# Splitting part of the weights into high and low parts by DMA

## The chip, the cores and the metric

One core of one Trainium2 chip. The metric is the device time of one execution in microseconds (us); lower is better. The engines are PE (matrix multiply), DVE (VectorE), ACT (ScalarE), POOL (GpSimd) and SP (SyncE, which here only issues DMAs). They run side by side, each takes its own instructions in a fixed order, and they wait for each other through semaphores.

## What is computed

One transformer layer over 512 tokens of width 1024. Of the reference, cut to what matters here:

```python
proj = rms_norm(x, g_mix) @ w_in
(q_n, kc_n, vc_n, ks_n, vs_n, kw_n, vw_n, gate_n,
 q_m, k_m, v_m, gate_a, gate_b) = jnp.split(proj, IN_CUTS, axis=-1)
y_nsa = nsa_mixer(q_n, kc_n, vc_n, ks_n, vs_n, kw_n, vw_n, gate_n, ...)
y_moba = moba_mixer(q_m, k_m, v_m, ...)
merged = sigmoid(gate_a) * (y_nsa @ w_up_nsa) + sigmoid(gate_b) * (y_moba @ w_up_moba)
x = x + merged @ w_out
gate, up = jnp.split(rms_norm(x, g_ffn) @ w_ffn_in, 2, axis=-1)
x = x + (silu(gate) * up) @ w_ffn_out
x = x + sigmoid(rms_norm(x, g_ple) @ w_ple_gate) * (p @ w_ple_proj)
```

All inputs are fp32. The weights that matter here are those of `gate_a` and `gate_b` (2048 columns of `w_in`; `ga` in the kernel) and `w_up_moba` (`um`).

## The kernel before

**Three products for one.** PE multiplies in fp32r, a shortened fp32. To keep the precision, each operand is split into a high part, the value rounded to fp32r, and a low part, the rest. A product is then high x high + low x high + high x low: `tmm` (L358 to L363) issues three matmuls of 128x128 weights by 512 tokens, L361 with the weights' high part `wh`, L362 with `wh` again and the activations' low part, L363 with the weights' low part `wl`.

**Weight units.** The weights come in 144 units of up to 128x1024 (512 KB), in the order of the list `units` (L206 to L219). Units 30 to 33 are `vm` (values of MoBA), 34 to 44 are `ga` 8 to 15 and 0 to 2, 45 to 48 are `um`, 49 to 53 are `ga` 3 to 7, 54 on are `un`. The class `Weights` (L54 to L101) prepares them: `load` issues a DMA on SP's queue into one of three `wr` buffers (L67), `parts` takes one of three `wh` and one of three `wl` buffers, writes `wh` with an ACT copy that rounds to fp32r (L84) and `wl = wr - wh` with a DVE subtraction (L85). `get` hands out the next unit, splits up to one unit ahead and loads up to five ahead.

**What runs beside what.** First come the projections in natural layout (`qm` to `vm`). Then attention (`attention`, L777) is woven with a filling of 20 units, 34 to 53: `gates` (L536) multiplies eight `tmm` per `ga` unit, ends in a DVE product (L541) and an ACT tanh (L542); `up` (L903) does the same for `um`. The weave (L933 to L937) gives 0.95 filling steps per attention step, later 0.65. An attention job has score matmuls (L790, L791), a DVE pass that masks and takes the bound (L793), the exponential on ACT (L795), a DVE or ACT scaling (L808, L810), transposes on PE (L818), a split of their result by ACT and DVE (L827, L828) and the product with the values (L837, L842). After it come the up projection of NSA, the output projection, the feed-forward part and the last gate.

**Order.** The program text gives priorities; the Tile framework, with `schedule_with_timeline_sim=True` (L1116), fixes the order of each engine's instructions when the program is built, from the priorities and a simulated timeline. So an instruction can stand earlier in its engine's queue than the text has it: ACT's copy into a `wh` buffer stands where the buffer comes free. Which unit an instruction belongs to is known from the built program, where the buffers are numbered (`wh34`) and whose order of matmuls the trace repeats; the trace itself leaves the numbers out.

```python
# L358 to L363, of tmm
T.matmul(o, wh[:, sl], h, start=start, stop=False)
T.matmul(o, wh[:, sl], l, start=False, stop=False)
T.matmul(o, wl[:, sl], h, start=False, stop=stop)
# L933 to L937
fill = chain(gates(8, 16), gates(0, BEFORE_UM), up("um", YM, up_moba_done), gates(BEFORE_UM, 8))
run(weave(weave(att, fill, *FILL_RATE), side, 0.2))
```

Of the kernel before, what the change touches and what calls it, by code (L numbers as in the profile page):

```python
# [10 lines left out]
F32 = mybir.dt.float32  # L11
F32R = mybir.dt.float32r
I32 = mybir.dt.int32
AF = mybir.ActivationFunctionType
OP = mybir.AluOpType
# [38 lines left out]
class Weights:  # L54
    def __init__(self, nc, pool, units):
        self.nc, self.pool, self.units = nc, pool, units
        self.raw, self.done = {}, {}
        self.n_raw = self.n_split = self.n_get = 0
        self.depth = 2

    def load(self, upto):
        while self.n_raw < min(upto, len(self.units)):
            i = self.n_raw
            src, n = self.units[i][1], self.units[i][2]
            t = self.pool.tile([128, 1024], F32, name=f"wr{i}", tag="wr", bufs=3)
            for a, b in self.pieces(i, n):
                self.nc.sync.dma_start(t[:, a:b], src[:, a:b])  # L67
            self.raw[i] = t
            self.n_raw += 1

    def pieces(self, i, n):
        return [(0, n // 2), (n // 2, n)] if i == 0 else [(0, n)]

    def parts(self):
        i = self.n_split
        self.load(i + 1)
        self.n_split += 1
        n = self.units[i][2]
        t = self.raw.pop(i)
        h = self.pool.tile([128, 1024], F32R, name=f"wh{i}", tag="wh", bufs=3)  # L80
        l = self.pool.tile([128, 1024], F32R, name=f"wl{i}", tag="wl", bufs=3)
        self.done[i] = (h, l)
        for a, b in self.pieces(i, n):
            self.nc.scalar.activation(h[:, a:b], t[:, a:b], AF.Copy)  # L84
            self.nc.vector.tensor_sub(l[:, a:b], t[:, a:b], h[:, a:b].bitcast(F32))  # L85
            yield
# [8 lines left out]
    def get(self, key):  # L95
        i = self.n_get
        assert self.units[i][0] == key, (self.units[i][0], key)
        self.n_get += 1
        self.split(i + self.depth)
        self.load(i + 6)  # L100
        return self.done.pop(i)  # L101

# [1018 lines left out]
```

## Time and profile before

| | |
|---|---|
| median of 3 runs | 863.8 us (863.54 to 864.02) |
| the profiled execution | 863.29 us |
| its span, first to last instruction | 861.4 us |
| busy: PE, DVE, ACT, POOL | 843.4, 532.2, 391.3, 139.2 us |
| HBM read | 79.64 MB |

PE is busy for 98% of the span. Matmuls are pipelined: one of 512 tokens has a record of some 390 ns, while the next starts some 230 ns after it. A wait is the idle time of an engine just before an instruction, with what released it. The stretch of the change is attention, about 160 to 376 us; the weights of units 34 to 36 are split before it, from 148 us on.

### The profile page before, as it was taken

Reading aid. Unit: us, or ns where it says so; the run is one execution under the profiler, and the core shown is the slowest. Engines: PE = TensorE matmul, PEld = TensorE weight load, DVE = VectorE, ACT = ScalarE, POOL = GpSimd, SP = SyncE. Lnnn points to the kernel's source line nnn. Section 1 sums busy time; section 2 is a strip of 40 time slices with the busy share of each in tenths; the row PEclk is TensorE's granted clock in tenths of the full one; section 3 lists DMA queues with packets and bytes.
Section 4 is the critical chain, followed back from the end, with each engine's and each line's share of the span. In section 5 each row is a group of like instructions: output and inputs, shape, how many; then the busy total and the mean of one; then the engine's idle time right before and its main releaser. Section 6 shows DMA issues by size and latency. Waiting matters only on the chain.

```text
span 861.4 us, 11012 instructions
## 1 busy us (share of the span) xinstructions
PE 843.4 (98%) x4169; PEld 708.5 (82%) x4169; DVE 532.2 (62%) x944; ACT 391.3 (45%) x708; POOL 139.2 (16%) x140
## 2 busy tenths in 40 slices
PE   9999999999999999999999999999999999999997
PEld 7878798888788888787888888888888888888886
DVE  6777766878976988749536555555555433233354
ACT  6455545877776877634423222233333222233421
POOL 2735443000000000024321111111111101010100
PEclk9999999999999999999999999999999999999999
DMA  9433525423211111116323333333323333333221
GB/s 328 153 99 98 162 73 142 129 64 89 84 49 50 50 49 36 63 49 216 102 76 121 98 98 97 99 98 97 95 91 94 84 109 87 93 110 97 98 99 49
DMA packets 26996, 85.58 MB, mean 99 GB/s; under 512 B 3392, under 2 KB 3904, under 8 KB 26944
## 3 DMA queue, kind: packets, MB, share of 16 engines
q1 hardware_dynamic: 26016, 82.78, 30.3%
q10 hardware_dynamic: 928, 2.11, 1.0%
q8 instruction: 32, 0.52, 0.3%
q14 instruction: 20, 0.16, 0.1%
HBM read 79.64 MB, written 2.10 MB: 95 GB/s over the span
## 4 chain that ended last, share of the span: by engine, by line
PE 84%; DVE 8%; ACT 2%; POOL 2%; DMA 2%; issue 1%; SPq 0%; DVEq 0%; ACTq 0%; POOLq 0%
PE fg L361 5%; PE fu L362 5%; PE fg L362 5%; PE fob L361 5%; PE fob L362 5%; PE fu L361 5%; PE fg L363 5%; PE fu L363 5%; PE fob L363 5%; PE ga L361 3%; PE ga L362 3%; PE ga L363 3%; PE pt L818 3%; DVE wl L85 2%; PE pgb L361 2%; PE pv L842 2%
## 5 line engine op out<-in xcount | busy, mean ns | idle before, releaser
L84 ACT ACTIVATE wh<-wr 128x1024 fp32r<-128x1024 f32 (+2 forms) x145 | 147.4, 1019 | 310.3 <-PE fu L362 73.6
L85 DVE TENSOR_TENSOR wl<-wr,wh 128x1024 fp32r<-128x1024 f32 (+2 forms) x145 | 196.2, 1357 | 106.0 <-ACT wh L84 105.4
L361 PE MATMUL fg<-x2h,wh 128*128 128x512 f32 x176 | 68.6, 390 | 0.0
L361 PE MATMUL fu<-x2h,wh 128*128 128x512 f32 x176 | 68.6, 390 | 0.0
L363 PE MATMUL fg<-x2h,wl 128*128 128x512 f32 x176 | 68.5, 389 | 0.0
L363 PE MATMUL fu<-x2h,wl 128*128 128x512 f32 x176 | 68.5, 389 | 0.0
L363 PE MATMUL fob<-HH,wl 128*128 128x512 f32 x176 | 68.5, 389 | 0.0
L362 PE MATMUL fu<-x2l,wh 128*128 128x512 f32 x176 | 68.5, 389 | 0.0
L362 PE MATMUL fg<-x2l,wh 128*128 128x512 f32 x176 | 68.5, 389 | 0.0
L362 PE MATMUL fob<-HL,wh 128*128 128x512 f32 x176 | 68.5, 389 | 0.0
L361 PE MATMUL fob<-HH,wh 128*128 128x512 f32 x176 | 68.5, 389 | 0.0
L1008 POOL TENSOR_TENSOR u<-zg,u 128x512 f32<-128x512 f32 x22 | 29.8, 1352 | 199.9 <-DVE u L1006 191.4
L361 PE MATMUL ga<-xh,wh 128*128 128x512 f32 x128 | 53.6, 419 | 0.0
L362 PE MATMUL ga<-xl,wh 128*128 128x512 f32 x128 | 50.3, 393 | 0.0
L363 PE MATMUL ga<-xh,wl 128*128 128x512 f32 x128 | 50.2, 393 | 0.0
L793 DVE CUSTOM_DVE_ANT_0 p<-sb,big_mask 128x512 f32<-128x512 f32 (+2 forms) x96 | 44.9, 484 | 7.3 <-PE sb L791 7.1
L1006 DVE SCALAR_TENSOR_TENSOR u<-fu,rb 128x512 f32<-128x512 f32 x22 | 15.2, 690 | 53.6 <-PE fu L363 53.6
L944 POOL TENSOR_TENSOR GT<-GT,GT 128x512 f32<-128x512 f32 x8 | 14.7, 1856 | 190.5 <-DVE GT L943 190.5
L245 POOL TENSOR_TENSOR ssum<-ssum,sqx 128x512 f32<-128x512 f32 x14 | 22.1, 1575 | 139.1 <-ACT sqx L244 139.1
L818 PE MATMUL pt<-ident,p 128*128 128x128 f32 x240 | 38.2, 274 | 2.8 <-DVE pw L828 2.7
L828 DVE TENSOR_TENSOR pw<-pt,pw 128x512 fp32r<-128x512 f32 x48 | 32.6, 684 | 10.7 <-ACT pw L827 10.3
L361 PEld LDWEIGHTS fu<-x2h,wh 128*128 128x128 f32 x176 | 33.1, 188 | 6.9
(590 smaller groups left out, 1993.5 us busy)
## 6 DMA issues: line engine op xcount, KB each, us to landing
wr<-fi SPq DMA_DIRECT2D x44, 512.0 KB, 3.4
wr<-ga SPq DMA_DIRECT2D x16, 512.0 KB, 3.5
wr<-fo SPq DMA_DIRECT2D x16, 512.0 KB, 3.5
wr<-wo SPq DMA_DIRECT2D x8, 512.0 KB, 3.6
wr<-pg SPq DMA_DIRECT2D x8, 512.0 KB, 3.4
wr<-fo SPq DMA_DIRECT2D x8, 384.0 KB, 3.2
xin<-xT SPq DMA_DIRECT2D x8, 256.0 KB, 5.5
xn<-xN SPq DMA_DIRECT2D x4, 512.0 KB, 7.8
```

Of the source, the lines that this page charges most:

```text
L84: self.nc.scalar.activation(h[:, a:b], t[:, a:b], AF.Copy)
L85: self.nc.vector.tensor_sub(l[:, a:b], t[:, a:b], h[:, a:b].bitcast(F32))
L245: G.tensor_tensor(ssum, ssum, q, op=OP.add)
L361: T.matmul(o, wh[:, sl], h, start=start, stop=False)
L362: T.matmul(o, wh[:, sl], l, start=False, stop=False)
L363: T.matmul(o, wl[:, sl], h, start=False, stop=stop)
L793: V.tensor_tensor_reduce(out=p, in0=o, in1=big_mask[:, 512 - n:512], op0=OP.add, op1=OP.min, scale=1.0, scalar=3.0e38, accum_out=st["m"][: ...
L818: last = T.transpose(b[:, off:off + 128], st["p"][:, P_OFF[qt] + kb * 128:P_OFF[qt] + kb * 128 + 128], ident)
L828: V.tensor_sub(pl, b[:, :off], ph.bitcast(F32))
L842: T.matmul(o, job["v"](kb), st.pop(("pl", kb))[:, cols], start=False, stop=job["last"] and kb == 2)
L1006: V.scalar_tensor_tensor(u, bu, 2.0, rb1, op0=OP.mult, op1=OP.mult)
L1008: G.tensor_tensor(u, zg, u, op=OP.mult)
```

## The change

For the units named `ga` and `um` (20 of 144, `by_dma`) `load` issues nothing. `fetch`, one unit further ahead than the split, takes the `wh` and `wl` buffers and issues a DMA on POOL's queue from the fp32 weights into the fp32r `wh`, which casts on the way. `parts` then writes `wl = -wh` with an ACT pass of the same size as the old copy, and issues a second DMA on POOL's queue that adds the weights to `wl` (`accum_op=OP.add`). The DVE subtraction is gone for these units. `get` calls `fetch` for one unit more than is split. `wr` buffers are no longer used by these units, so later units can be loaded into them earlier.

```diff
@@ class Weights
     def load(self, upto):
         while self.n_raw < min(upto, len(self.units)):
             i = self.n_raw
+            if self.by_dma(i):
+                self.n_raw += 1
+                continue
...
+    def by_dma(self, i):
+        return i < len(self.units) and self.units[i][0][0] in ("ga", "um")
+
+    def fetch(self, upto):
+
+        while self.n_high < min(upto, len(self.units)):
+            i = self.n_high
+            if self.by_dma(i):
+                src, n = self.units[i][1], self.units[i][2]
+                h = self.pool.tile([128, 1024], F32R, name=f"wh{i}", tag="wh", bufs=3)
+                l = self.pool.tile([128, 1024], F32R, name=f"wl{i}", tag="wl", bufs=3)
+                self.nc.gpsimd.dma_start(h[:, :n], src)
+                self.high[i] = h, l
+            self.n_high += 1
+
     def parts(self):
         i = self.n_split
+        if self.by_dma(i):
+            self.fetch(i + 1)
+            self.n_split += 1
+            src, n = self.units[i][1], self.units[i][2]
+            h, l = self.done[i] = self.high.pop(i)
+            self.nc.scalar.activation(l[:, :n], h[:, :n].bitcast(F32), AF.Copy, scale=-1.0)
+            self.nc.gpsimd.dma_start(l[:, :n], src, accum_op=OP.add)
+            yield
+            return
         self.load(i + 1)
         self.n_split += 1
+        self.n_high = max(self.n_high, i + 1)
...
         self.split(i + self.depth)
+        self.fetch(self.n_split + 1)
         self.load(i + 6)
```

## Rows read from the trace of the kernel before

**Rows 1.** The page's busy times: engine, us, share of the span, instructions.
```profile
PE 843.4 (98%) x4169; PEld 708.5 (82%) x4169; DVE 532.2 (62%) x944; ACT 391.3 (45%) x708; POOL 139.2 (16%) x140
```
**Rows 2.** Busy time by stretch, 148 to 376 us; the first line names the columns.
```profile
core 0: us, PE busy (x) PEld busy (x) DVE busy (x) ACT busy (x) POOL busy (x), PEclk, DMA share, GB/s
...
180.00:200.00 20.00, 19.44 (x112) 16.30 (x111) 17.88 (x54) 14.70 (x34) 0.74 (x1) 1.00 0.27 80
...
sum 228.00, PE 223.44 PEld 190.18 DVE 180.53 ACT 162.72 POOL 2.22; mean PE 18.62 PEld 15.85 DVE 15.04 ACT 13.56 POOL 0.18
```
**Rows 3.** PE's waits, 160 to 376 us: waiter, releaser, us in total, times, longest.
```profile
PE pt L818 <- DVE pw L828: 2.7, 5, 1.5
PE sb L790 <- DVE am__2543 L793: 0.6, 1, 0.6
PE sb L790 <- DVE am__1754 L793: 0.5, 1, 0.5
PE sb L790 <- DVE am__3097 L793: 0.4, 1, 0.4
```
**Rows 4.** Instructions by line and form, 160 to 376 us, of DVE and ACT.
```profile
L85 DVE TENSOR_TENSOR wl<-wr,wh 128x1024 fp32r<-128x1024 f32 x20 | 24.4, 1218 | 2.5 <-ACT wh L84 2.4
...
L84 ACT ACTIVATE wh<-wr 128x1024 fp32r<-128x1024 f32 x20 | 21.1, 1055 | 10.5 <-PE ga L362 10.5
```
**Rows 5.** Timeline of PE, the matmuls behind four waits: start, us, what, [idle before].
```profile
160.03 0.50 PE L790 MATMUL sb<-KM,QM 128*128 128x512 f32 x1 [0.45 <-DVE am__1754 L793]
...
196.19 0.41 PE L818 MATMUL pt<-ident,p 128*128 128x128 f32 x2 [0.56 <-DVE pw L828]
...
234.55 0.41 PE L818 MATMUL pt<-ident,p 128*128 128x128 f32 x2 [1.45 <-DVE pw L828]
...
252.66 0.66 PE L818 MATMUL pt<-ident,p 128*128 128x128 f32 x4 [0.32 <-DVE pw L828]
```
**Rows 6.** Timeline of DVE ahead of those four waits.
```profile
158.29 1.22 DVE L85 TENSOR_TENSOR wl<-wr,wh 128x1024 fp32r<-128x1024 f32 x1
...
188.49 1.23 DVE L85 TENSOR_TENSOR wl<-wr,wh 128x1024 fp32r<-128x1024 f32 x1
...
230.10 0.69 DVE L770 TENSOR_TENSOR yf<-pv,yt 64x512 f32<-64x512 f32 x1 [0.37 <-ACT yt L766]
...
248.86 1.22 DVE L85 TENSOR_TENSOR wl<-wr,wh 128x1024 fp32r<-128x1024 f32 x1
```
**Rows 7.** DMAs: issue (ns min/median/max, us), time to landing (us), size.
```profile
L67 SPq DMA_DIRECT2D wr<-ga x10: 327/328/328, 168.7 to 307.2; - x10
...
DMA to landing us min/median/max: 3.2/3.3/4.5
...
169.22 0.51 ACTq L454 DMA_DIRECT2D k2M<-KM  x1
...
k2M<-KM ACTq DMA_DIRECT2D x4, 256.0 KB, 4.3
```
**Rows 8.** Timeline of POOL, its longest instruction between 140 and 200 us.
```profile
146.15 1.65 POOL L393 TENSOR_TENSOR hf__1532<-ss__1531,half_neg 128x8 f32<-128x8 f32 x1 [9.32 <-DVE ss__1531 L392]
```
**Rows 9.** Timeline of ACT, the copies into `wh` of units 34, 37 and 38.
```profile
148.20 1.06 ACT L84 ACTIVATE wh<-wr 128x1024 fp32r<-128x1024 f32 x1 [0.30 <-PE vm L353]
...
166.39 1.06 ACT L84 ACTIVATE wh<-wr 128x1024 fp32r<-128x1024 f32 x1
...
177.07 1.06 ACT L84 ACTIVATE wh<-wr 128x1024 fp32r<-128x1024 f32 x1 [0.88 <-PE ga L362]
```
**Rows 10.** Timeline of PE, the first matmul with `wl` of units 34, 37 and 38.
```profile
161.20 0.39 PE L363 MATMUL ga<-xh,wl 128*128 128x512 f32 x1
...
182.62 0.39 PE L363 MATMUL ga<-xh,wl 128*128 128x512 f32 x1
...
191.53 0.39 PE L363 MATMUL ga<-xh,wl 128*128 128x512 f32 x1
```
**Rows 11.** One line of the source, L810: one job's three scalings, ns min/median/max.
```profile
L810 DVE TENSOR_SCALAR p<-p,as__2839 x3: 285/347/414, 265.1 to 265.5; 128x128 f32<-128x128 f32 x1, 128x256 f32<-128x256 f32 x1, 128x384 f32<-128x384 f32 x1
```

## What the change should do to the time

> **What bounds the kernel now.** I read the busy times first: PE is busy for 843.4 of 861.4 us [rows 1], so only 18 us of the whole span can be won by shortening waits. The change touches 20 weight units (numbers 34 to 53 in the list `units`), all used beside attention. The second view is the table by stretch [rows 2]: at 180 to 200 us DVE is busy for 17.88 of 20 us, ACT for 14.70, POOL for 0.74, the DMA engines for a share of 0.27, and the granted clock is 1.00, so the clock is no part of this. PE is nevertheless the engine that lacks time: from 148 to 376 us it is busy for 223.44 of 228.00 us. The third view lists what PE waited for there [rows 3]: 2.7 + 0.6 + 0.5 + 0.4 = 4.2 us, every piece released by a DVE instruction. That is the ceiling of what a relieved DVE can give back.
>
> **What it removes.** Per unit, one load into `wr` on SP's queue, one ScalarE copy into `wh` and one VectorE subtraction into `wl`. A subtraction takes 1218 ns [rows 4], so 20 of them are 24.4 us of DVE time. What of it lies on the path? I went to each wait of PE and looked back along DVE to the last moment at which DVE stood idle. Three waits have a `wl` subtraction in the unbroken run that leads to them: 0.45 us at 160.03, 0.56 at 196.19 and 0.32 at 252.66 [rows 5], with the subtractions at 158.29, 188.49 and 248.86 [rows 6]. Each wait is shorter than the 1.2 us taken out ahead of it, so each goes: 0.45 + 0.56 + 0.32 = **1.3 us**. The longest wait, 1.45 us at 234.55 [rows 5], has none in its run, which starts at 230.10 behind ACT's `yt` [rows 6]; I leave it standing. What is late next is the same DVE work without the subtraction (score bounds at L793, products at L828), and PE itself. So the gain lies between 0 and 4.2 us; I take 1.3 because that part has its cause in the rows. SP loses 20 issues of loads that were there ahead of their use; nobody waits for that.
>
> **What it adds.** ScalarE keeps one pass per unit: `l = -h` over 128x1024 replaces `h = w` over 128x1024, 1055 ns each [rows 4]; net zero, and no gain, since the shape is the same. POOL gets two DMA issues per unit, 40 in all. The cast and the addition each read 512 KB from HBM where one load did: 20 x 512 KB = 10.5 MB more, over a stretch of some 200 us in which the DMA engines have three quarters of their time free [rows 2].
>
> The price is delay. Before, `wh` of a unit is written as soon as its buffer (one of three) is free, and `wl` right behind it. After: the buffer is free, POOL issues the cast, it lands, ACT writes `l`, POOL issues the addition, it lands. Nothing in this trace is issued by POOL, casts or adds, so each term has two ends:
> - An issue on POOL: 0.33 us is what SP's takes, 0.51 what ACT's takes [rows 7], 1.65 POOL's longest instruction near there [rows 8]. I take 0.5, the nearest in kind.
> - The cast: a plain 512 KB load lands after 3.2 us at best and 3.3 at the median; above, a load and an on-chip copy one after the other, 3.3 + 4.3 = 7.6 us [rows 7]. I take 3.3, since it reads and writes what the plain load does.
> - The addition must also read its destination: the same ends, and I take the middle, 5.4, as neither row is nearer.
> - ACT's pass: 1.06.
>
> Sum: 0.5 + 3.3 + 1.06 + 0.5 + 5.4 = **10.8 us**. With the lower ends it is 0.33 + 3.2 + 1.06 + 0.33 + 3.2 = 8.1, with the upper ends 1.65 + 7.6 + 1.06 + 1.65 + 7.6 = 19.6.
>
> How long may it take? From the moment the buffer is free to the unit's first matmul with `wl` (L363). ACT's pass of before starts when the buffer comes free, so its start marks the first of these. For unit 34 that is 148.20 to 161.20: **13.0 us**; for unit 37, 166.39 to 182.62: 16.2; for unit 38, 177.07 to 191.53: 14.5 [rows 9, 10]. The other 17, worked out in the same way, have 15.9 us or more. So 10.8 us is hidden everywhere, with 2.2 to spare at unit 34, and 19.6 is not. Where the cover is gone, PE stands at L363 until the addition lands.
>
> POOL's queue is in order: an addition waits there for ACT, and behind it stands the next unit's cast. That cast needs a buffer that comes free about 10 us after the one before (166.39, 177.07 [rows 9]), so it loses nothing. POOL's own work in the stage is 0.74 us at 180 to 200 [rows 2] and the tail of the projections at 146.15 [rows 8]. In ACT's queue the pass now waits for a landing, and behind it stand the exponentials and evacuations of attention: that is the first rival.
>
> There is one more thing on DVE that POOL's issues could meet: scaling the probabilities (L810) takes 285, 347 and 414 ns for 128, 256 and 384 columns [rows 11], so some 65 ns per further 128 columns, where a `wl` subtraction takes 1218 / 8 = 152 per 128 [rows 4]. The three add up to 1.05 us, once per attention job. If each held one POOL issue back by its whole length, both issues of a unit would make the chain 10.8 + 2.1 = 12.9 us, still inside 13.0. The Trainium skill, SBUF — State Buffer, section "SBUF: two separate sides", says that POOL can't write a DMA's descriptors while DVE works in a mode that uses two ports, and gives about 620 ns for a transfer alone against 3100 ns beside such work. By that, as an estimate 2.5 us more per transfer, the chain would be 15.8 us; no run here shows it yet.
>
> **Against the clock of the runs.** The profiled execution took 863.29 us, 1.9 more than its span, and the median of the runs is 863.8. Forecast: 863.29 - 1.3 = 862.0 for such an execution, 863.8 - 1.3 = **862.5** for the median.
>
> **Rivals.**
> - *ACT stands.* The order on each engine is fixed when the program is built, by a planner that assumes a landing time for the cast. If the chip's is later by d, ACT stands d at each of 20 passes with the exponentials behind it, and PE waits for those. For it: ACT is busy for 14.70 of 20 us [rows 2], so it has about 2.7 us free per unit of some 10. Against it: the buffer comes free 13 us or more before the unit is due, so the pass need not be early in the queue. With d = 1 us ACT loses 20 us; between none and all of it reaches PE, half is 10: 863.8 - 1.3 + 10 = 872.5, slower. It decides from 3.0 us reaching PE, a d of 0.3 us.
> - *The addition lands late.* From a chain of 13.0 us on, PE waits at unit 34. At the upper end: 19.6 - 13.0 = 6.6 there, 19.6 - 16.2 = 3.4 at unit 37, 19.6 - (14.5 + 3.4) = 1.7 at unit 38: 11.7 us, 874.2, and some more at units of 16 to 17 us. For it: adding is the one operation without a near row. Against it: 2.2 us to spare at the tightest place, 3.7 and more elsewhere.
> - *DVE holds POOL up*, at 2.5 us per issue in place of the 1.05 of the rows: 15.8 - 13.0 = 2.8 at unit 34 and 15.8 - 14.5 = 1.3 at unit 38, 863.8 - 1.3 + 4.1 = 866.6. The rows speak against it: no run of L810 is that long.
> - *All DVE waits go.* With 24 us less on DVE the planner may place the rest so that all of [rows 3] vanishes: 863.8 - 4.2 = 859.6.
>
> That the change doesn't do what it says would be a cast that copies the bits as they are: then `l` is zero and the time is that of the forecast, since every instruction still runs.
>
> **How the numbers follow.** Chances: forecast 0.47 (own range 861 to 864), ACT stands 0.27, addition late 0.13, DVE holds POOL up 0.05, all waits go 0.08. A measurement of this kernel can tell about 0.2% from no change, 1.7 us. The forecast's 1.3 us is inside that: of its 0.47, 0.36 is "same", 0.10 faster (a little more than 1.3 won) and 0.01 slower. ACT stands: 0.22 slower, 0.05 same. Addition late: 0.10 slower, 0.03 same. DVE holds POOL up: slower. All waits go: faster. Together: faster 0.18, same 0.44, slower 0.38. The range, 860.3 to 873, leaves out the full gain of 4.2 us (0.06), the upper part of ACT's case (0.08) and of the late addition (0.05).
>
> **What would show it.** In the changed trace: no `wl` subtraction for `ga` and `um`, 24 us less DVE, and PE's waits for DVE in the stage down from 4.2 to about 2.9 us. ACT's pass waiting for a DMA, with PE idle behind exponentials, is the first rival; PE waiting for a DMA at L363 the second; long POOL issues beside L810 the third. I am wrong if the two landings of a unit add up to more than 11 us, or if ACT's waits for the casts sum to more than 6 us.

## The result: 868.9 us, 0.56% slower, and the profile after

| | before, same chip | after |
|---|---|---|
| median | 863.7 us | 868.9 us (868.61 to 869.94) |
| ratio to before, 95% interval | 1 | 1.0056 (1.0040 to 1.0072) |
| span of the profiled execution | 861.4 us | 866.7 us |
| HBM read | 79.64 MB | 90.13 MB |

The forecast was 862.5 with a range to 873.0. The time is inside the range, but on the other side of before. The stage of the change, from the first `ga` unit to the last, holds the whole loss: what follows it runs 5.3 us later than before, in unchanged spacing, to the end.

Page of after, the busy times and the two new DMAs (512 KB each; the last column is the us from issue to landing):

```profile
PE 846.3 (98%) x4169; PEld 709.6 (82%) x4169; DVE 511.9 (59%) x924; ACT 390.7 (45%) x708; POOL 168.4 (19%) x180
...
wh<-ga POOLq DMA_DIRECT2D x16, 512.0 KB, 3.9
wl<-ga POOLq DMA_DIRECT2D x16, 512.0 KB, 5.4
```

Against [rows 1] DVE has 20 instructions and 20 us less, POOL 40 instructions more, ACT the same number; 10.5 MB more are read. So the change does what it says.

PE's waits in after, 160 to 376 us, the stretch of [rows 3], with all the rest that the view shows:

```profile
PE pv L866 <- ACT pw L856: 2.9, 1, 2.9
PE ga L392 <- DMA wl<-ga: 1.3, 1, 1.3
PE pt L847 <- DVE PC L758: 0.7, 1, 0.7
PE pt L847 <- DVE pw L857: 0.6, 3, 0.2
PE sb L819 <- DVE am__2529 L822: 0.4, 1, 0.4
PE sb L819 <- DVE am__3747 L822: 0.4, 1, 0.4
PE sb L819 <- DVE am__3580 L822: 0.2, 1, 0.2
PE pt L847 <- DVE as__2530 L832: 0.2, 1, 0.2
PE sb L819 <- DVE am__2097 L822: 0.2, 1, 0.2
```

The seven rows released by DVE sum to 2.7 us where [rows 3] has 4.2. Two rows are new: 2.9 us behind ACT, once, and 1.3 us behind a DMA, once. ACT's own waits for the casts, same stretch:

```profile
ACT wl L99 <- DMA wh<-ga: 7.8, 9, 2.4
ACT wl L99 <- DMA wh<-um: 0.5, 1, 0.5
```

A stand is the time in which ACT waits for a cast with its next work queued behind. Timelines of after: ACT at its two long stands, and from the second of them to L856, the split of attention's transposed probabilities; then PE's wait for that, and PE's other new wait:

```profile
223.98 1.06 ACT L99 ACTIVATE wl<-wh 128x1024 fp32r<-128x1024 f32 x1 [2.35 <-DMA wh<-ga]
...
234.06 1.06 ACT L99 ACTIVATE wl<-wh 128x1024 fp32r<-128x1024 f32 x1 [2.06 <-DMA wh<-ga]
235.02 0.61 ACT L801 ACTIVATE YMh<-yf 128x512 fp32r<-128x512 f32 x1
235.54 0.49 ACT L824 ACTIVATE p<-p,am__2529 128x256 f32<-128x256 f32 x1
...
236.53 1.09 ACT L856 ACTIVATE pw<-pt 128x512 fp32r<-128x512 f32 x2
...
237.19 0.62 PE L866 MATMUL pv<-pw,VM 128*128 128x512 f32 x1 [2.87 <-ACT pw L856]
...
161.40 0.50 PE L392 MATMUL ga<-xh,wl 128*128 128x512 f32 x1 [1.27 <-DMA wl<-ga]
```

The passes at 223.98 and 234.06 are those of units 42 and 43. Behind the second are queued a copy (L801), two exponentials (L824) and then the copy L856 that PE waits for. The first, though it stood longer, has no wait of PE behind it: PE was busy for all of 217 to 228 us. The stretch that holds this, by windows (columns as in [rows 2]):

```profile
220.00:240.00 20.00, 16.50 (x86) 13.64 (x85) 13.96 (x43) 12.71 (x29) 2.30 (x3) 0.94 0.67 142
240.00:260.00 20.00, 19.29 (x107) 16.39 (x107) 12.83 (x37) 14.57 (x33) 2.83 (x4) 0.98 0.40 86
```

The granted clock, 1.00 in every such window of before, is 0.94 and then 0.98. The record of the clock behind it: half (1.2 for 2.4 GHz) for 3.4 us from 237.4 on, that is, from 0.2 us after the end of PE's 2.87 us of idle. Work lost there: (0.06 + 0.02) x 20 = 1.6 us. Before is not free of this: of its 20 executions beside the first four experiments, 12 have a mean granted clock of 0.998 and a mean span 1.6 us longer than the six at 1.00, so the 1.6 us lost here is not in full a loss against before's median.

The whole attention stage of both, 140 to 385 us (before, then after):

```profile
140.00:385.00 245.00, 240.24 (x1314) 203.94 (x1314) 188.67 (x517) 171.59 (x402) 5.84 (x8) 1.00 0.21 65
...
140.00:385.00 245.00, 237.27 (x1290) 200.15 (x1289) 165.78 (x492) 168.43 (x399) 32.72 (x46) 0.99 0.48 108
```

So of the 5.3 us, 240.24 - 237.27 = 3.0 is idle of PE, 1.6 the half clock, and 0.7 remains, which was not traced further (the matmuls come in another order, at other spacings).

### The profile page after: what moved, and what is told of

Read it like the earlier page. It is cut to its first block, busy times and chain, and to the rows that moved or that the text cites. A ratio compares the mean times of both kernels' runs of the same rounds, so it can differ in the third digit from the quotient of the medians.

```text
span 866.7 us, 11013 instructions
## 1 busy us (share of the span) xinstructions
PE 846.3 (98%) x4169; PEld 709.6 (82%) x4169; DVE 511.9 (59%) x924; ACT 390.7 (45%) x708; POOL 168.4 (19%) x180
## 3 DMA queue, kind: packets, MB, share of 16 engines
HBM read 90.13 MB, written 2.10 MB: 106 GB/s over the span
## 4 chain that ended last, share of the span: by engine, by line
PE 79%; DVE 6%; issue 6%; DMA 4%; POOL 3%; ACT 2%; SPq 0%; POOLq 0%; DVEq 0%; ACTq 0%
PE fg L390 5%; PE fg L392 5%; PE fu L392 5%; PE fob L391 5%; PE fu L391 5%; PE fg L391 5%; PE fob L390 5%; PE fob L392 5%; PE fu L390 5%; PE pt L847 2%; PE ga L392 2%; PE ga L390 2%; PE ga L391 2%; PE pgb L390 2%; PE pgb L392 2%
## 5 line engine op out<-in xcount | busy, mean ns | idle before, releaser
L112 ACT ACTIVATE wh<-wr 128x1024 fp32r<-128x1024 f32 (+3 forms) x125 | 126.3, 1014 | 304.6 <-PE fu L391 69.5
L113 DVE TENSOR_TENSOR wl<-wr,wh 128x1024 fp32r<-128x1024 f32 (+3 forms) x125 | 171.7, 1378 | 105.3 <-ACT wh L112 104.9
L392 PE MATMUL fg<-x2h,wl 128*128 128x512 f32 x176 | 68.5, 389 | 0.0
L392 PE MATMUL fu<-x2h,wl 128*128 128x512 f32 x176 | 68.5, 389 | 0.0
L392 PE MATMUL fob<-HH,wl 128*128 128x512 f32 x176 | 68.5, 389 | 0.0
L392 PE MATMUL ga<-xh,wl 128*128 128x512 f32 x128 | 50.6, 396 | 1.3 <-DMA wl<-ga 1.3
L391 PEld LDWEIGHTS fg<-x2l,wh 128*128 128x128 f32 x176 | 33.1, 188 | 6.9
L390 PEld LDWEIGHTS fob<-HH,wh 128*128 128x128 f32 x176 | 33.0, 188 | 6.9
```

## The experiments

Each ran beside before on the same chip; ratios are to that. Three theories stand behind the expectations: **A**, ACT stands at the cast's landing; **B**, the planner's new order costs it, whatever lands when; **C**, the low parts land late.

**The passes on POOL.** In `parts`:

```diff
-self.nc.scalar.activation(l[:, :n], h[:, :n].bitcast(F32), AF.Copy, scale=-1.0)
+self.nc.gpsimd.tensor_scalar(l[:, :n], h[:, :n].bitcast(F32), -1.0, None, op0=OP.mult)
```

> The changed kernel, but l = -h is made by POOL instead of ACT, so that no instruction of ACT waits for a cast. Theory A (ACT stands at the landing of the cast: 2.06 us at 234 us, PE 2.9 us idle behind it, then half clock for 3.4 us): ACT's waits for DMA go from 8 us to 0, the 2.9 us wait and the clock drop go, 20 passes of 1.06 us leave ACT; 862 to 865 us. Theory B (the planner's new order of the instructions is the cause, whatever lands when): 867 to 870. Theory C (the addition lands late): a POOL pass is slower than ACT's, so PE's wait for wl grows from 1.3 us, at unit 34 first; 868 to 872.

Measured: 869.8 us, ratio 1.0063 (1.0049 to 1.0077). The profile is of the slowest of six executions, 873.1 us. POOL's passes and PE's waits, 160 to 376 us:

```profile
L99 POOL TENSOR_SCALAR wl<-wh 128x1024 fp32r<-128x1024 f32 x18 | 49.8, 2769 | 93.9 <-DMA wh<-ga 23.2 <-issue 20.0 <-PE pt L847 15.2
...
PE ga L392 <- DMA wl<-ga: 4.4, 4, 2.3
PE pt L847 <- DVE pw L857: 2.9, 5, 1.5
```

ACT no longer stands for casts, and the 2.9 us wait behind it is gone (0.9 us behind another ACT instruction, L475, is new). But a pass takes POOL 2.77 us for ACT's 1.06; pass, addition and the next cast share one in-order queue; and now PE waits for low parts, 4.4 us at units 34, 37, 38 and 41. The clock falls all the same, for 3.4 us from 231.3, within the 2.3 us wait for the low part of unit 41. The time lies in the ranges of both B and C, and C's sign is there. One wait took the place of another, so the run doesn't separate A from B; it shows that low parts that land later are late at four units.

**The pass one exponential later.** The pass is ordered behind the last exponential ahead of it in the program:

```diff
...
+with self.tc.issue_after(self.marks[-1]) if len(self.marks) >= 1 else nullcontext():
     self.nc.scalar.activation(l[:, :n], h[:, :n].bitcast(F32), AF.Copy, scale=-1.0)
```

> The changed kernel, with ACT's pass for a unit queued behind the last exponential that the program has ahead of it; in ACT's queue it stands up to four exponentials later than before, two later at units 42 and 43. Theory A: the casts have landed when ACT comes to them, its waits for DMA at units 42 and 43 go from 4.4 us to under 1, PE's 2.9 us wait and the clock drop go; 864 to 866 us. Theory B: 867 to 870. Theory C: the additions start later by 1 to 4 us, PE waits for wl at more units; over 869.

Measured: 866.5 us, ratio 1.0033 (1.0023 to 1.0044). ACT's waits for casts, then PE:

```profile
ACT wl L101 <- DMA wh<-ga: 1.7, 2, 0.9
...
235.29 0.50 PE L869 MATMUL pv<-pw,VM 128*128 128x512 f32 x1 [2.25 <-ACT pw L859]
236.69 0.41 PE L850 MATMUL pt<-ident,p 128*128 128x128 f32 x2 [0.89 <-DVE pw L860]
```

The stands fall from 8.3 to 1.7 us and (0.0056 - 0.0033) x 864 = 2.0 us come back; the time lies between A's range and B's. Not all came back: a pass of 1.06 us with 0.71 of stand ahead of it still lies at 233.04, in front of the copies that PE needs, PE is idle for 2.25 us, and the clock is at half for 3.4 us from 237.0.

**The relief alone.** Before without the subtractions; no `wl` buffer is taken for these units, and their third product reads `wh`:

```diff
-self.nc.vector.tensor_sub(l[:, a:b], t[:, a:b], h[:, a:b].bitcast(F32))
...
+if self.units[i][0][0] not in ("ga", "um"):
+    self.nc.vector.tensor_sub(l[:, a:b], t[:, a:b], h[:, a:b].bitcast(F32))
```

> The kernel before, without the subtraction of the 20 units (their third product is made with the high part in place of the low part); no DMA on POOL, no wait for one. It measures what a DVE relieved of 24 us gives by itself. My prediction's term: 1.3 us, so 862.4. If all waits of PE for DVE in the stage go: 859.5. If relief gives nothing, or the planner's order eats it: 863.7 or more, and then part of the 5.3 us loss has nothing to do with DMAs.

Measured: 860.8 us, ratio 0.9963 (0.9951 to 0.9975). PE's waits, 160 to 376 us:

```profile
PE sb L792 <- DVE am__2525 L795: 0.7, 1, 0.7
PE sb L792 <- DVE am__3727 L795: 0.5, 1, 0.5
PE ga L363 <- ACT QN L448: 0.5, 1, 0.5
PE pt L820 <- DVE pw L830: 0.4, 2, 0.2
```

The relief is worth 0.0037 x 864 = 3.2 us, not 1.3, and of this 2.1 are waits of PE (4.2 less 2.1, the sum of the rows). Where the rest comes from wasn't traced; the free `wl` buffers are part of it, and so is the clock of before's executions. The 1.45 us wait of [rows 5] is gone as well. So, if the relief is worth as much in after, what the change adds costs 3.2 + 4.8 = 8.0 us (0.0056 x 864 = 4.8 by the ratio; 5.3 between the profiled spans).

**All but units 42 and 43.** These two are split as before:

```diff
-return i < len(self.units) and self.units[i][0][0] in ("ga", "um")
+return i < len(self.units) and self.units[i][0][0] in ("ga", "um") and i not in (42, 43)
```

> The changed kernel, with units 42 and 43 (the two at which ACT stood for over 2 us) split by ACT and DVE as before. Theory A: PE's 2.9 us wait and the half clock behind it go, the rest stays; 864 to 866 us. Theory B: 867 to 870. If the stand only moves to the units next to them: 866 to 868, with ACT waiting for a cast there.

Measured: 864.7 us, ratio 1.0009 (1.0001 to 1.0018). Waits of ACT and PE, 160 to 376 us:

```profile
ACT wl L99 <- DMA wh<-ga: 9.4, 7, 3.2
...
PE pv L866 <- ACT pw L856: 1.3, 2, 0.7
PE ga L392 <- DMA wl<-ga: 1.1, 1, 1.1
```

Most of the loss went with two units of twenty, and so did the half clock. ACT's stands sum to more than in after, the longest to 3.2 us (unit 37, at 172 us), and cost PE little: no wait over 0.3 us follows that one. What counts is not how long ACT stands but where: in after, unit 43's stand is at the changeover from MoBA's last products (`VM`) to NSA's first scores (`KN`), where PE has no other matmul queued ahead of those that need ACT's copy. Before has its longest wait at the same place (234.55 [rows 5]). The two units also have their subtractions back on DVE, and the order is another; the run doesn't part these from the stands.

**No pass at all.** `wl` comes by a second casting DMA:

```diff
-self.nc.scalar.activation(l[:, :n], h[:, :n].bitcast(F32), AF.Copy, scale=-1.0)
-self.nc.gpsimd.dma_start(l[:, :n], src, accum_op=OP.add)
+self.nc.gpsimd.dma_start(l[:, :n], src)
```

> Leaves out ScalarE's negating pass in the 20 units: wl is fetched as a second casting DMA of the weights, not added to -wh, so wl holds the weights themselves and the low products are of that. Everything else as after. ScalarE has nothing left to wait for in these units. A (ScalarE stands at the cast's landing, and the pass itself is 20 x 1.06 us in its queue): the stands and TensorE's idle behind them go, no stretch at half clock near 235 us, and the relief of VectorE shows: 860.5 to 863 us, ratio 0.9965 to 0.9995. B (the planner's new order alone costs it, whatever lands when): 866 to 869 us. C (the low parts land late): they land some 5 us earlier than with the pass, so the wait of 1.1 to 1.3 us at unit 34 goes as well, but only that: 867 to 868 us.

Measured: 862.95 us, ratio 0.999 (0.9981 to 0.9999). PE's two longest groups of waits, 160 to 376 us:

```profile
PE pt L846 <- DVE pw L856: 2.1, 4, 1.5
PE sb L818 <- DVE am__2092 L821: 0.9, 1, 0.9
```

With as many bytes read into the same tiles and no ACT pass, the loss is gone, and no stretch of attention is at half clock. The addition is gone with the pass, so the two are not tried apart. It is no 860.8 either: PE's waits sum to 4.0 us, near before's 4.2, with the 1.5 us at L846 (that of 234.55 before) among them. Whether traffic, POOL's issues or the order keeps the remaining 2 us stays open.

**Casts one unit earlier.** A fourth `wh` buffer (the big pool gives one up), and:

```diff
-BIG_BUFS = 36
+BIG_BUFS = 35
...
-h = self.pool.tile([128, 1024], F32R, name=f"wh{i}", tag="wh", bufs=3)
+h = self.pool.tile([128, 1024], F32R, name=f"wh{i}", tag="wh", bufs=4)
...
-self.fetch(self.n_split + 1)
+self.fetch(self.n_split + 2)
```

(the second edit at both places that take a `wh`).

> After, with a fourth buffer for the high parts (the big pool has 35 buffers for 36) and the cast issued one unit sooner, so it lands some 10 us before the pass is queued. A: ScalarE's waits for casts, 8.3 us in after, fall under 2 us; no idle of TensorE over 2 us behind an exponential, no half clock near 235 us; 863.5 to 866 us, ratio 0.999 to 1.002, the rest being the extra pass's place in the queue and the start at unit 34. B: as after, 867.5 to 870. C: the additions are issued when the passes are, so they land earlier too by what the passes no longer stand; the wait at unit 34 stays at 1.1 to 1.3 us.

Measured: 862.3 us, ratio 0.998 (0.9969 to 0.999). ACT's waits of the pass, 160 to 376 us, and its passes at the changeover:

```profile
ACT wl L99 <- PE ga L392: 7.0, 9, 1.4
ACT wl L99 <- DMA wh<-ga: 1.4, 1, 1.4
ACT wl L99 <- PE umo L392: 1.3, 2, 1.0
...
217.72 1.06 ACT L99 ACTIVATE wl<-wh 128x1024 fp32r<-128x1024 f32 x1 [1.39 <-PE ga L392]
227.96 1.06 ACT L99 ACTIVATE wl<-wh 128x1024 fp32r<-128x1024 f32 x1 [0.66 <-PE ga L392]
239.40 1.06 ACT L99 ACTIVATE wl<-wh 128x1024 fp32r<-128x1024 f32 x1 [0.84 <-PE ga L392]
```

The casts have landed when the passes come up, save at the start: the stands for DMAs fall from 8.3 to 1.4 us in this stretch. What the pass waits for now is its `wl` buffer, which PE's products release and no DMA. PE's only wait at the changeover is 0.7 us. At units 35 and 36 ACT still stands, 0.93 us ahead of 154.95 and 1.36 ahead of 158.98; PE waits 1.05 us behind ACT at 160.71, and the clock is at half for 3.4 us from 160.7. The time is below A's range and below before's; whose gain that is, the last controls say.

**The subtraction on POOL.** Before, with:

```diff
-self.nc.vector.tensor_sub(l[:, a:b], t[:, a:b], h[:, a:b].bitcast(F32))
+eng = self.nc.gpsimd if self.units[i][0][0] in ("ga", "um") else self.nc.vector
+eng.tensor_tensor(l[:, a:b], t[:, a:b], h[:, a:b].bitcast(F32), op=OP.subtract)
```

> Before, with the 20 subtractions done by GpSimd and not by VectorE; loads, rounding on ScalarE and all else as before. GpSimd took 1.86 us for a subtraction-like 128x512 in before, so about 3.7 us for 128x1024 against VectorE's 1.22. A (only ScalarE's standing cost after its gain): the chain load, rounding, subtraction has no landing in ScalarE's queue that is new, and its low part comes 2.5 us later than before, inside the 13 us between a buffer's release and its use: 860.3 to 862.5 us, ratio 0.9955 to 0.9985, near e3_no_sub's 860.8. Rival (GpSimd is too slow, as in e1_neg_on_pool where its pass took 2.8 us): low parts late, TensorE waits for wl by over 2 us in all, 865 us or more.

Measured: 872.6 us, ratio 1.0097 (1.0081 to 1.0114). A fell, and the rival had the time but not the reason. POOL needs 2.39 us, less than assumed, and PE waits for no low part. But seven DVE instructions took 1.5 to 2.7 us that elsewhere take 0.15 to 0.69, each while a subtraction ran on POOL; they sum to 12.3 us too much (three more took 0.6 to 1.1). One of them, and the same instruction of another job:

```profile
231.57 2.38 POOL L86 TENSOR_TENSOR wl<-wr,wh 128x1024 fp32r<-128x1024 f32 x1 [9.17 <-ACT wh L84]
231.76 2.74 DVE L721 TENSOR_TENSOR CD<-CD,cu__2447 128x512 f32<-128x512 f32 x1
...
L721 DVE TENSOR_TENSOR CD<-CD,cu__2176 x1: 694/694/694, 200.2 to 200.2; 128x512 f32<-128x512 f32 x1
```

L721 starts 0.19 us after POOL's subtraction and ends 0.55 us after it, about its own length: it stood until POOL was done. The Trainium skill, SBUF — State Buffer, section "Who interferes with whom", says that a DVE instruction with two inputs in SBUF shares its second read path with a POOL instruction that reads SBUF. The trace agrees: 2.74 us beside, 0.69 without. But L801, a DVE instruction with one input (128x4), was held too, 1.53 us for 0.17. PE's waits in the stretch sum to 9.1 us for before's 4.2, 7.6 of them released by DVE, and the clock is at half for 3.4 us from 238.4; how much of that is the 12.3 us was not tried apart.

**Units 34 to 36 as before.** The condition of `by_dma` gets `and i >= 37`.

> After, with units 34 to 36 split as before (loads by SP, rounding, VectorE's subtraction) and only units 37 to 53 by DMAs. It takes away the cast of unit 34 that is issued too late for its use (TensorE waited 1.3 us for its low part) and the crowd of five swaps and casts in the queues there. A: the stands of units 42 and 43 stay, so of the 5.3 us only 1 to 1.5 go: 867 to 868.5 us, ratio 1.0035 to 1.0055. C (late low parts and the crowd at the start are the larger loss, and delay all behind them): 864 to 866 us. B: an order of its own, no forecast.

Measured: 867.3 us, ratio 1.0036 (1.0024 to 1.0049). The wait for the low part of unit 34 is gone, and 1.7 us come back (0.0056 - 0.0036 = 0.0020 of 864), a little more than A's 1 to 1.5. The long stands stay at units 42 and 43 (the sixth and seventh of the 17 passes), as A had it, and PE's wait behind the second with them:

```profile
222.34 1.06 ACT L99 ACTIVATE wl<-wh 128x1024 fp32r<-128x1024 f32 x1 [2.44 <-DMA wh<-ga]
...
232.46 1.06 ACT L99 ACTIVATE wl<-wh 128x1024 fp32r<-128x1024 f32 x1 [2.19 <-DMA wh<-ga]
...
235.59 0.79 PE L866 MATMUL pv<-pw,VM 128*128 128x512 f32 x1 [2.99 <-ACT pw L856]
```

The time lies in A's range. So the crowd of transfers at the start isn't what makes ACT stand there.

**Controls for the buffers.** After, and before, with `BIG_BUFS = 35` alone:

> After with one buffer fewer in the big pool (35 for 36), as e6_four_wh has it, and nothing else changed: a control for e6. A (what e6 gained came from the earlier cast): about as after, 867 to 870 us, ratio 1.004 to 1.007, with one idle of TensorE over 2 us and a stretch at half clock near 235 us. Rival (the other pool size alone puts the work in a better order): 862 to 864.5 us.

> Before with one buffer fewer in the big pool, nothing else changed: a control for e6 against before. A: within 0.2% of before, 862.2 to 865.7 us. Rival (the pool size alone gains): 861 us or less, and e6's gain over before is then not the change's.

Measured: after 869.0 us, ratio 1.0052 (1.0039 to 1.0064), with the same wait behind ACT and half clock for 3.4 us from 238.1; before 864.4 us, ratio 1.0001 (0.9990 to 1.0012). Of PE's waits in the first:

```profile
PE pv L866 <- ACT pw L856: 2.9, 1, 2.9
```

The pool's size changes neither time by more than the intervals.

**Both edits together**, the earlier casts and `i >= 37`:

> e6_four_wh with units 34 to 36 split as before (loads by SP, subtraction on VectorE) and units 37 to 53 by DMAs: the two parts that cost in after, the cast that lands when it is queued and the crowd of casts and swaps at the start, are both out. A: ScalarE's standing at 154.95 and 158.98 us (0.93 + 1.36 us in e6) goes, and with it TensorE's 1.05 us at 160.7 and the 3.4 us at half clock behind it, some 1 + 1.7 us less than e6: 859.5 to 861.5 us, ratio 0.995 to 0.9975. Rival (the start costs nothing that is not given back, or the order is another one): 862 to 865 us.

Measured: 861.0 us, ratio 0.9967 (0.9954 to 0.998), as A had it: ACT stands for no cast, and the wait and the half clock at 160.7 are gone. But the 1.4 us wait of before at the changeover is back, and 1.1 us of the lead over before is there at 140 us, ahead of the change.

**Before with the fourth `wh` buffer** (the `bufs=4` and `BIG_BUFS` lines of the earlier casts, nothing else):

> Before with the fourth buffer for the high parts (and 35 buffers in the big pool), as e6 and e11 have them, the weights loaded, rounded and subtracted as before: a control for e11. e11's trace is already 1.3 us ahead of before's at 147 us, before the first unit of the change, in an order that differs from 28 us on; that part would come from the buffer. A (the earlier cast made the gain in attention): 861.5 to 863.5 us, ratio 0.9965 to 0.999, e11 still 1 us or more below it. Rival (the buffer alone gives it, the DMAs add nothing): 860 to 861.3 us, as e11.

Measured: **859.7 us, ratio 0.9958 (0.9945 to 0.9972)**. The rival holds, a little below its range: the buffer alone gives all that the two kernels with DMAs gained over before. PE's waits, 160 to 376 us, with every subtraction still on DVE:

```profile
PE sb L790 <- DVE am__2543 L793: 1.2, 1, 1.2
PE pt L818 <- DVE pw L828: 0.8, 4, 0.2
PE sb L790 <- DVE am__3765 L793: 0.6, 1, 0.6
```

This is the lowest time of the kernels here (e11's and e3's intervals overlap with it), and it beats both before and after. 0.5 us of the gain is there at 140 us, and PE's waits in the stretch sum to 2.6 us for 4.2; why a fourth buffer gives the rest isn't shown. The right comparison for the earlier casts is with it: 0.998 / 0.9958 = 1.0022, by the two intervals about 1.0005 to 1.0039. With four buffers on both sides the change of all 20 units still costs, 1.9 us in place of 4.8. For the kernel with both edits it is 0.9967 / 0.9958 = 1.0009, about 0.9990 to 1.0028: with units 34 to 36 left as before, neither a cost nor a gain can be told.

## Why the prediction was wrong

**Right.** The durations held. The two landings are 3.9 and 5.4 us at the page's median, for 3.3 and 5.4 in the sum; POOL's issues 0.56 (cast) and 0.86 us (addition), for 0.5. ACT's work stayed level. The chain hid at 19 units of 20. PE's waits for DVE in the stretch fell to 2.7 us, for 2.9 forecast, but that is luck: the 1.45 us at 234.55, which was to stand, is replaced there by the 2.87 behind ACT, and others came, 0.71 at 258.95 the longest. POOL lost nothing beside L810 (L839 in after): six of its issues ran beside that line, at 0.85 to 0.87 us (addition) and 0.56 to 0.57 (cast), as alone. The 2.5 us per issue, an estimate from the figures of the Trainium skill, SBUF — State Buffer, section "SBUF: two separate sides", show nowhere at these 0.3 to 0.4 us instructions.

**Wrong: which case is the likeliest.** The step that failed is the argument against "ACT stands": "the buffer comes free 13 us or more before the unit is due, so the pass need not be early in the queue". It need not, but it was. In after 15 of the 20 passes start within 0.1 us of their cast's landing, and 10 have it as what they waited for. By this the planner put each pass at the landing that it assumed, ahead of work that PE wants sooner; its own timeline stands in no trace, so this is inferred. The slack of the unit, which I had worked out with care, was the wrong quantity; the place in an in-order queue was the right one. My own mark for this, ACT's waits for casts above 6 us, came to 8.3.

**The price of that rival** had the right size by a wrong way. It took half of ACT's standing to reach PE, evenly spread: 10 us at d = 1 us. The measured d is 8.3 / 20 = 0.4 us, half of it 4.2. But PE lost 2.9 us at one place and next to nothing at the others, and in e4, with 9.7 us of standing (9.4 and 0.3 for `um`) elsewhere, it waited 1.3 us for ACT. So the size is luck. To the 2.9 comes a term that the prediction excluded by "the clock is no part of this": 1.6 us at half clock behind that wait. A row of before can't exclude what a new idle of PE brings, and some executions of before show a lowered clock too.

**The relief was mis-sized**: 1.3 us forecast, 3.2 measured alone (e3). Looking for a subtraction in the unbroken run ahead of each wait missed the 1.45 us at 234.55, which went too. In e5 and e11, also without most subtractions, it is back; so the order seems to decide it, which wasn't tried apart. So such a wait can be counted neither as lost nor as won from one trace; the rival "All DVE waits go" had 4.2.

**The late addition**: mechanism right, at one unit. The chain of unit 34 took 161.36 - 148.73 = 12.6 us for 10.8, since its cast took 5.4 us beside other transfers. The cover was not 13.0 but less: PE, relieved, came to L392 at 161.40 - 1.27 = 160.13, a microsecond sooner than before. It cost 1.3 us of wait, which is gone in e8. The landings of a unit summed to more than 11 us five times (up to 13.8 at unit 35), my mark for being wrong, but PE came later than the low part to all five; unit 34, with 10.8, was the only one it waited for.

**Order (B)** is not out as a part. e5 returned to before's time, not to e3's, and has no ACT stands: these 2 us aren't settled, since traffic, POOL's issues and order were not separated. e6 against e12 still shows 1.9 us, but e6 has 1.05 us of wait behind ACT's stands at the start and 1.7 us of half clock there (0.5 x 3.4); e11, without these, can't be told from e12.

## What to carry to other kernels

When a step is moved behind a DMA, the question is not whether the unit has time, but where the consumer of the landing stands in its engine's in-order queue, what is queued behind it, and whether PE has other work at that moment. A transfer that is issued a unit ahead costs a buffer and takes the stand away; try that buffer on the unchanged kernel first, as it may be the whole gain. And a wait of PE is dearer than its length if the clock falls behind it.

## What the hardware showed that was not expected

- **The clock.** In after it fell to half for 3.4 us from 237.4, with 2.87 us of idle just ended; in e2 for 3.4 us from 237.0, after 2.25; in e8 for 6.8 us from 234.6, around 2.99. In e7 it fell for 3.4 us from 238.4, with 1.05 and 1.15 us of idle ended at 236.0 and 238.4. In before 0.56 and 1.45 us within three microseconds left it at full, as 0.45 and 1.46 did in e5; in e6 it fell for 3.4 us from 160.7 after 1.05 us and two of 0.35 before it. In e6 and e12 it also fell from 48 us on, ahead of the change, with 1.7 to 1.9 and 1.0 us of idle; 1.4 and 1.0 at the same place left it at full in e11. The longest single idle doesn't decide alone.
- **A cast beside other transfers.** Alone it lands 3.5 to 4.1 us after its issue. With another cast, the addition of the unit before it or the swaps of attention in flight it took 5.0 to 6.6 (6.1 and 5.6 at units 42 and 43, in e8 6.2 and 5.8 there), but 4.1 at unit 41, beside the addition of unit 40. Additions took 5.2 to 6.2, and 7.4 to 8.8 three times.
- **POOL and DVE** (e7): a DVE instruction of 0.69 us took 2.74 beside a subtraction on POOL. In e1, where POOL's pass has one input, the longest such case was 1.2 us for one of 0.41 (L839, 128x384).
